# Two transformer blocks on one core: links between sublayers as one task of three parts, first group of the latent columns whole, weight sums in place

## The chip, the cores and the metric

The kernel runs on one core of one Trainium2 chip. The metric is the time of one execution on the device in microseconds (us), as the median of several runs. The engines are named as the profile names them: PE is TensorE (PEld its weight loads), DVE VectorE, ACT ScalarE, POOL GpSimd, SP SyncE.

## What is computed

The reference runs two blocks one after the other. The first holds two hybrid layers on 512 latent columns and 256 context columns of width 1024. Each layer is a feed-forward sublayer, a mixer (two kinds of attention and a Fourier transform between an input and an output projection), and a second feed-forward sublayer. Every sublayer takes the norm of its input, modulates it, and adds its normed and gated output to the input:

```python
def rms_norm(x, g):
    y = x32 * lax.rsqrt(jnp.mean(x32 * x32, axis=-1, keepdims=True) + RMS_EPS)
    return (y * g.astype(jnp.float32)).astype(x.dtype)

def ffn_sublayer(h, m, sub, g_pre, g_post, w1, w2):
    shift, scale, gate = mods_of(m, sub)
    y = swiglu(modulate(rms_norm(h, g_pre[sub]), shift, scale), w1, w2)
    return h + MACARON_WEIGHT * gate * rms_norm(y, g_post[sub])

def hybrid_layer(x, xc, mod, mod_c, ...):
    x = ffn_sublayer(x, mod, 0, g_pre, g_post, w_ffn_in[0], w_ffn_out[0])
    xc = ffn_sublayer(xc, mod_c, 0, g_pre, g_post, w_ffn_in[0], w_ffn_out[0])
    ...
    h = modulate(rms_norm(x, g_pre[1]), sh, sc)
    hc = modulate(rms_norm(xc, g_pre[1]), shc, scc)
    ...
    x = x + gt * rms_norm(o, g_post[1])
    x = ffn_sublayer(x, mod, 2, g_pre, g_post, w_ffn_in[1], w_ffn_out[1])
```

In the second layer the context ends after the mixer's input projection, which makes only keys and values of it. The second block (a linear recurrence with a state-space scan, then a stick-breaking attention) works on the latent columns and is not touched.

## The kernel before

Activations lie transposed: 128 features on the partitions, columns side by side, eight tiles for the width of 1024. The context columns are a stream named `cx` (256 columns, on the left), the latent ones `lat` (512), which is also cut into its halves `la` and `lb` (256 each). A float32 product is three matmuls (`mm3`, L421 to L423), of operands split in a high and a low part: ScalarE copies the high part (L347), VectorE or GpSimd subtracts it from the value (L353). Weights come through `raw` buffers (four, by DMA) and are split into `op` buffers (eight).

A feed-forward sublayer (`ffn`, named here by layer and place: 00, 02, 10, 12) goes through the hidden features in groups of 4, 4, 4, 3, 3 and 4 blocks. `ffn1` makes a group's hidden block (`mid`), `ffn2` adds its product to the output `Y`. In the first group ffn1 runs for cx, then for la, then for lb, each with its own load and split of the weights, because the columns of a sublayer come ready in that order. From the second group on, ffn1 of all 768 columns is done by a Strassen step over halves of 384 columns (`strassen`), seven products instead of eight; `wsums` makes the sums of weight blocks that it needs, four adds on VectorE for each block, into two buffers named `ws` and back into `raw`. The column sums that Strassen needs (`Halves`: `sums`, `third`) are made on VectorE and GpSimd beside the end of the first group. In the last group ffn2 runs for cx, then for lat.

Between two sublayers lies a link for each stream: `post` (norm of the output, gate, residual; L507, L509) and `pre` (norm of the new input, modulation and split; L525 to L527). Each of them calls `rstd`: two small matmuls of 128 x 1 sum the squares of 256 columns (L463), VectorE works out the reciprocal root on 128 x 2 values in 13 small steps (L474 to L482) and spreads it as a diagonal `dg` (L484), and two matmuls with it (L489) bring it to all partitions. The squares are added up by `add_sq` (L450) in a tile `ss`.

What order these pieces have on an engine is set when the program is built, by a small planner, `run`: tasks are generators that yield after each piece the time that it is thought to take (positive: TensorE's time, which moves the clock; negative: a time after which the task may go on). `run` takes next the first task whose time has come, the critical ones ahead of the fill. It returns when all are done (`drain`). The link of cx runs beside ffn2 of lat; the link of lat (at the borders into the mixers one link of 512 columns, at those out of the first mixer and of 02 the halves la and lb) runs in the next sublayer beside its first work on cx: ffn1 and ffn2 of the first group, or the mixer's context projections. TensorE runs its instructions in the order written; so does each other engine.

## Time and profile before

| | us |
|---|---|
| median of 3 runs | 3797.84 |
| the three runs | 3793.26 to 3799.57 |
| the profiled execution | 3801.48 |
| its span in the trace | 3799.7 |
| PE, DVE, ACT, POOL busy in it | 3504.7, 2364.0, 1708.1, 1400.0 |

The span is that of one execution seen by the hardware profiler, and the profiled execution's own time is some 2 us longer. "Busy" is the time in which an engine has an instruction under way, over the whole program; stretches with different limits are mixed in it, so that the sections below look at single borders between sublayers. PEclk in the rows is the clock granted to TensorE as a share of full speed: 1.00 is 2.4 GHz, 0.50 is 1.2 GHz.

### The profile page before, as it was taken

What the parts mean: (1) busy time and instruction counts of PE and PEld (TensorE: products, weight loads), DVE (VectorE), ACT (ScalarE), POOL (GpSimd) and SP (SyncE); (2) the same over time, 40 slices, a digit from 0 to 9 for tenths busy, and PEclk for the clock granted to TensorE, in tenths of its full rate; (3) what the DMA queues carried; (4) which work ended last, traced back from release to release, by engine and by line L of the source; (5) the groups of instructions that cost most, each with busy time, mean ns of one, the idle gap of its engine ahead of it and who ended that gap; (6) DMA issues with size and microseconds to landing.
All of it is one profiled execution on the core that took longest, in us unless ns stands there. A gap on an engine that the chain in (4) does not pass through costs nothing.

```text
span 3799.7 us, 61164 instructions
## 1 busy us (share of the span) xinstructions
PE 3504.7 (92%) x23260; PEld 3128.4 (82%) x23260; DVE 2364.0 (62%) x4769; ACT 1708.1 (45%) x3599; POOL 1400.0 (37%) x1151
## 2 busy tenths in 40 slices
PE   7899998998979999988999979888998898999997
PEld 5788897777878888888889967688887877999886
DVE  5844458667784444786445586667567776555546
ACT  5433334456543323454323445554444635635544
POOL 4533343211344333345333431145555433333112
PEclk8999998999989999999999989999999989999998
DMA  7433424212344343443342321242333311234112
GB/s 270 136 125 128 136 75 142 91 56 86 118 127 134 122 134 122 145 145 98 126 138 72 129 91 51 69 133 80 101 99 118 119 44 48 76 116 136 60 48 76
DMA packets 125437, 410.38 MB, mean 108 GB/s; under 512 B 14035, under 2 KB 25814, under 8 KB 123350
## 3 DMA queue, kind: packets, MB, share of 16 engines
q1 hardware_dynamic: 125142, 406.47, 33.5%
q8 instruction: 182, 2.98, 0.3%
q14 instruction: 113, 0.93, 0.1%
HBM read 397.90 MB, written 8.52 MB: 107 GB/s over the span
## 4 chain that ended last, share of the span: by engine, by line
PE 53%; DVE 15%; issue 5%; ACT 5%; POOL 2%; DMA 1%; ACTq 0%; DVEq 0%; POOLq 0%; SPq 0%
PE pg L421 9%; PE pg L422 9%; PE pg L423 9%; PE bank L416 7%; PE bank L421 4%; PE bank L423 3%; PE bank L422 3%; DVE op L353 2%; DVE ss L450 1%; PE po L611 1%; POOL op L353 1%; ACT op L347 1%; PE po L844 1%; PE psw L868 1%; PE po L1830 1%
## 5 line engine op out<-in xcount | busy, mean ns | idle before, releaser
L353 POOL TENSOR_TENSOR op<-raw,op 128x512 fp32r<-128x512 f32 (+1 forms) x660 | 891.2, 1351 | 1488.2 <-ACT op L347 1259.1
L347 ACT CAST op<-raw 128x512 fp32r<-128x512 f32 (+2 forms) x1178 | 709.9, 606 | 821.8 <-PE pg L423 421.3
L353 DVE TENSOR_TENSOR op<-raw,op 128x512 fp32r<-128x512 f32 (+2 forms) x518 | 402.6, 779 | 224.2 <-ACT op L347 217.7
L421 PE MATMUL pg<-h,op 128*128 128x256 f32 (+1 forms) x1440 | 480.1, 333 | 61.7 <-DVE m L758 26.5
L422 PE MATMUL pg<-h,op 128*128 128x256 f32 (+1 forms) x1440 | 467.9, 325 | 4.6 <-DVE h L527 3.3
L423 PE MATMUL pg<-h,op 128*128 128x256 f32 (+1 forms) x1440 | 462.3, 321 | 1.0 <-DVE op L353 0.6
L421 PE MATMUL pg<-mid,op 128*128 128x512 f32 (+1 forms) x1106 | 386.3, 349 | 13.6 <-ACT mid L347 5.3
L422 PE MATMUL pg<-mid,op 128*128 128x512 f32 (+1 forms) x1106 | 379.2, 343 | 1.8 <-DVE mid L353 1.7
L423 PE MATMUL pg<-mid,op 128*128 128x512 f32 (+1 forms) x1106 | 378.8, 342 | 0.0
L421 PEld LDWEIGHTS pg<-h,op 128*128 128x128 f32 x1440 | 293.6, 204 | 86.7 <-DVE m L758 29.2
L422 PEld LDWEIGHTS pg<-h,op 128*128 128x128 f32 x1440 | 292.7, 203 | 23.2 <-DVE h L527 11.1
L423 PEld LDWEIGHTS pg<-h,op 128*128 128x128 f32 x1440 | 293.1, 204 | 16.0 <-DVE op L353 1.0
L416 PE MATMUL bank<-h,op 128*128 128x384 f32 (+1 forms) x1704 | 293.5, 327 | 9.4 <-DVE u L704 9.4
L353 POOL TENSOR_TENSOR op<-ws,op 128x512 fp32r<-128x512 f32 x142 | 191.7, 1350 | 276.8 <-ACT op L347 276.8
L416 PEld LDWEIGHTS bank<-h,op 128*128 128x128 f32 x1704 | 280.9, 190 | 12.3 <-DVE u L704 12.3
L421 PEld LDWEIGHTS pg<-mid,op 128*128 128x128 f32 x1106 | 208.4, 188 | 75.0 <-DVE y L788 29.2
L788 DVE TENSOR_TENSOR y<-pg,y 128x256 f32<-128x256 f32 (+1 forms) x252 | 141.1, 562 | 198.2 <-PE pg L423 197.6
L422 PEld LDWEIGHTS pg<-mid,op 128*128 128x128 f32 x1106 | 208.6, 189 | 27.0 <-DVE mid L353 3.5
L423 PEld LDWEIGHTS pg<-mid,op 128*128 128x128 f32 x1106 | 208.3, 188 | 26.1
L421 PE MATMUL bank<-h,op 128*128 128x384 f32 (+1 forms) x636 | 206.4, 324 | 0.0
L423 PE MATMUL bank<-h,op 128*128 128x384 f32 (+1 forms) x636 | 203.6, 320 | 0.0
L422 PE MATMUL bank<-h,op 128*128 128x384 f32 (+1 forms) x636 | 203.6, 320 | 0.0
(434 smaller groups left out, 8430.1 us busy)
## 6 DMA issues: line engine op xcount, KB each, us to landing
raw<-wf SPq DMA_DIRECT2D x326, 512.0 KB, 3.7
mraw<-wmod SPq DMA_DIRECT2D x128, 512.0 KB, 4.7
raw<-win SPq DMA_DIRECT2D x58, 512.0 KB, 3.7
raw<-ewin SPq DMA_DIRECT2D x48, 512.0 KB, 3.6
raw<-owin SPq DMA_DIRECT2D x40, 512.0 KB, 3.6
raw<-wout SPq DMA_DIRECT2D x32, 512.0 KB, 3.6
raw<-wf SPq DMA_DIRECT2D x32, 384.0 KB, 3.2
raw<-ewout SPq DMA_DIRECT2D x24, 512.0 KB, 3.6
```

The source lines that it names most:

```text
L347: self.nc.scalar.copy(hi, src)
L353: eng.tensor_tensor(out=lo, in0=src, in1=hi.bitcast(F32), op=ALU.subtract)
L416: mm = self.nc.tensor.matmul if not more else lambda *a, **kw: self.nc.tensor.matmul(*a, skip_group_check=True, **kw)
L421: mm(p, lhsT=a, rhs=xh, start=start and i == 0, stop=False)
L422: mm(p, lhsT=a, rhs=xl, start=False, stop=False)
L423: mm(p, lhsT=b, rhs=xh, start=False, stop=stop and i == len(rhs) - 1)
L450: (eng or self.nc.vector).tensor_tensor(out=st.s, in0=st.s, in1=q, op=ALU.add)
L611: nc.tensor.matmul(box["po"][32 * j : 32 * j + 32, :], lhsT=self.cT[:, k, :], rhs=raws[j // 2][:, 512 * (j % 2) : 512 * (j % 2) + 512], st ...
L788: nc.vector.tensor_tensor(out=y, in0=p, in1=y, op=ALU.add)
L844: self.nc.tensor.matmul(o[64 * h : 64 * h + 64, :P], lhsT=cur["v"][h][c], rhs=pTs[h][:, c * P : (c + 1) * P], start=c == 0, stop=c == nt - 1)
L868: nc.tensor.matmul(S[:, h, col : col + ap.shape[1]], lhsT=q[h], rhs=ap, start=True, stop=True)
L1830: nc.tensor.matmul(o[64 * h : 64 * h + 64, :P], lhsT=vt[:m, t, 64 * h : 64 * h + 64], rhs=wTs[h][:m, t, :], start=t == 0, stop=t == j + 1)
```

## The change

Five things change together.

1. **Links as one task.** The links of cx, la and lb become one task, one after the other (`links`). It starts beside the last products of the sublayer and is carried over the border into the next one: `run` gets an `until`, with which it returns as soon as the fill is done and leaves the critical task where it stands. Notes order it: a link waits for the note "y" of its stream, set behind the stream's last product; the next sublayer's first work waits for the note "hcx", set behind cx's link.
2. **Last group in three parts.** ffn2 of the last group, and the first mixer's output projection, run for cx, la, lb (256 columns each) instead of cx, lat. So la's link may start beside lb's products. All links are of 256 columns now, into the mixers too.
3. **First group's latent part whole.** ffn1 of the first group runs for cx and then for all 512 latent columns at once, so that its weights are loaded and split twice instead of three times. At the start of the program the norm of the latent input is of 512 columns as well.
4. **Weight sums in place.** `wsums` writes three of its four sums over the weights in `raw` and one into a single `ws`.
5. **Small things.** Sum-of-squares tiles of up to 384 columns get buffers of their own (`sh`, 3), the wide ones one (`ss`); the 512-wide gate tile comes from the general buffers; the rotary tables are loaded when the first latent half is done with, or at the end of the entry.

The sublayer 12, the second block, and the exits from the second mixer keep their form. Line numbers of the helpers go down by one (L421 to L420, L463 to L462, L489 to L488).

```diff
-    def run(self, crit, fill=(), drain=True):
+    def run(self, crit, fill=(), drain=True, until=None):
         tasks = [t if isinstance(t, Task) else Task(t) for t in (*crit, *fill)]
-        must = tasks if drain else tasks[: len(crit)]
+        must = tasks[len(crit) :] if until else tasks if drain else tasks[: len(crit)]
         for t in tasks:
-            t.t = self.clock
+            t.t = max(t.t or 0, self.clock)
...
     def stile(self, n):
-        return self.tmp.tile([P, 512], F32, name="ss", tag="ssum", bufs=NSS)[:, :n]
+        return self.tmp.tile([P, 512], F32, name="ss", tag="ssum", bufs=1)[:, :n] if n > 384 else self.tmp.tile([P, 272], F32, name="sh", tag="sh", bufs=NSS)[:, :n]
...
         o1 = put(a11, True)
-        s1, s2 = tmp(), tmp()
+        s1 = self.fpool.tile([P, 512], F32, name="ws", tag="ws", bufs=1)
         add(s1, a21, a22)
         o2 = put(s1, True)
-        add(s2, s1, a11)
-        o3 = put(s2, False)
         add(a21, a11, a21)
+        add(a11, s1, a11)
+        o3 = put(a11, False)
         o4 = put(a21, True)
         o5 = put(a12, False)
-        add(s2, s2, a12)
-        o6 = put(s2, True)
+        add(a12, a11, a12)
+        o6 = put(a12, True)
         o7 = put(a22, True)
...
                 if first:
-                    self.run(pend[:1], [self.chain(g1(firsts[:1]), *([g2(firsts[:1], False)] if len(firsts) > 2 else []))])
-                    for i in range(1, len(firsts) - 1):
-                        self.run(pend[i : i + 1], [g1(firsts[i : i + 1], t=l == sub == 0)])
+                    self.run([pend], [self.chain(*([self.wait_for("hcx"), g1(firsts[:1]), g2(firsts[:1], False)] if full else [g1(firsts[:1])]))])
...
                     else:
-                        for i in range(len(lasts)):
-                            self.run(exits[i - 1 : i], [g2(lasts[i : i + 1], False, spill and not i and (lambda: spill(False)))])
+                        self.run([g2(lasts[:1], False, lambda: spill(False))])
+                        links = self.links(lasts, exits)
+                        self.run([links], [self.chain(*[x for st in lasts[1:] for x in (g2([st], False), self.mark(st, "y"))])], until=True)
+                        return links
...
+    def links(self, ss, exits):
+        self.known.pop("hcx", None)
+        self.yfree = False
+        def go():
+            for i, (st, e) in enumerate(zip(ss, exits)):
+                if i:
+                    yield from self.wait_for((st, "y"))
+                    del self.known[st, "y"]
+                yield from e
+                if not i:
+                    self.note("hcx")
+        return Task(go())
...
-            self.run([entry()], [proj(cx, [0, 1, 2, 7, 5, 6, 3, 4])])
+            self.run([entry()], [self.chain(self.wait_for("hcx"), proj(cx, [0, 1, 2, 7, 5, 6, 3, 4]))])
...
-                self.run(exits[:1], [o_proj(lat)])
+                links = self.links([cx, *lasts], exits)
+                self.run([links], [self.chain(*[x for st in lasts for x in (o_proj(st), self.mark(st, "y"))])], until=True)
+                return links
...
-        first = [cx, la, lb]
-        pend = [self.chain(self.square_x(st), self.pre(st, 0, 0)) for st in (la, lb)]
-        pend = self.ffn(0, 0, first, [lat], both, both, pend, links(0, 0, 0, 1), lambda out: spill(out, True), first=loads)
+        self.note("hcx")
+        pend = Task(self.chain(self.square_x(lat), self.pre(lat, 0, 0)))
+        pend = self.ffn(0, 0, both, [lat], both, parts, pend, links(0, 0, 0, 1), lambda out: spill(out, True), first=loads)
```

How this moves the instructions is seen in three places. The first is TensorE at the border from 02 to 10. Before, `bank<-ones,ss` and `bank<-dg,ones` are the sums and the diagonal of a norm, `h_122` to `h_129` the eight tiles of the new input (256 wide: context or one latent half), and `op` the weights. Around the sums of lb's first norm, and then (behind "...") around lb's second norm, stands:

```order
L423 MATMUL pg<-h_125,op 128x256
L421 MATMUL pg<-h_126,op 128x256
L422 MATMUL pg<-h_126,op 128x256
L423 MATMUL pg<-h_126,op 128x256
L463 MATMUL bank<-ones,ss 128x1 x2
L421 MATMUL pg<-h_127,op 128x256
L422 MATMUL pg<-h_127,op 128x256
L423 MATMUL pg<-h_127,op 128x256
...
L421 MATMUL pg<-h_129,op 128x256
L422 MATMUL pg<-h_129,op 128x256
L423 MATMUL pg<-h_129,op 128x256
L463 MATMUL bank<-ones,ss 128x1 x2
L489 MATMUL bank<-dg,ones 128x128 x2
L421 MATMUL pg<-h_122,op 128x256
```

Now the rows around lb's two norms on TensorE at the same border are these (`mid` is the context's hidden block, of ffn2):

```order
L420 MATMUL pg<-mid,op 128x256
L421 MATMUL pg<-mid,op 128x256
L422 MATMUL pg<-mid,op 128x256
L462 MATMUL bank<-ones,sh 128x1 x2
L420 MATMUL pg<-mid,op 128x256
L421 MATMUL pg<-mid,op 128x256
L422 MATMUL pg<-mid,op 128x256
L488 MATMUL bank<-dg,ones 128x128 x2
L462 MATMUL bank<-ones,sh 128x1 x2
L488 MATMUL bank<-dg,ones 128x128 x2
L420 MATMUL pg<-h_122,op 128x512
L421 MATMUL pg<-h_122,op 128x512
```

Before, la's first-group products (`h`, 128x256) stand around and between lb's norms; now three context products stand within the first norm and nothing behind it, and the next latent product, 512 wide, follows lb's second diagonal.

The second place is TensorE at the entry into the second mixer. Before, the end of the context projections and the norm of all 512 latent columns (`psw`, four matmuls each), with transposed values (`pt`) between, is:

```order
L950 MATMUL pt<-ident,vt 128x128 x2
L421 MATMUL pg<-h_129,op 128x256
L422 MATMUL pg<-h_129,op 128x256
L423 MATMUL pg<-h_129,op 128x256
L950 MATMUL pt<-ident,vt 128x128 x2
L463 MATMUL psw<-ones,ss 128x1 x4
L489 MATMUL psw<-dg,ones 128x128 x4
L421 MATMUL pg<-h_122,op 128x512
L422 MATMUL pg<-h_122,op 128x512
```

Now there are three norms of 256 columns in the same place, la's second and lb's two, the last two of which have nothing in front of them:

```order
L982 MATMUL pt<-ident,vt 128x128 x2
L420 MATMUL pg<-h_129,op 128x256
L421 MATMUL pg<-h_129,op 128x256
L422 MATMUL pg<-h_129,op 128x256
L488 MATMUL psw<-dg,ones 128x128 x2
L982 MATMUL pt<-ident,vt 128x128 x2
L462 MATMUL psw<-ones,sh 128x1 x2
L488 MATMUL psw<-dg,ones 128x128 x2
L462 MATMUL psw<-ones,sh 128x1 x2
L488 MATMUL psw<-dg,ones 128x128 x2
L420 MATMUL pg<-h_122,op 128x512
```

The latent projection (`h_122`, 128x512) follows directly behind lb's two norms, where one norm stood directly ahead of it before.

The third place is VectorE in two Strassen steps of the first sublayer. Before, the adds of `wsums` (L393) read `ws` and `raw` and write `ws` mostly, beside sums of results (L788) and splits (L353):

```order
L393 TENSOR_TENSOR ws_4361<-raw_4355 128x512
L393 TENSOR_TENSOR raw_4355<-raw_4354,raw_4355 128x512
L788 TENSOR_TENSOR y2_132<-pg_4040,y2_132 128x256
L788 TENSOR_TENSOR y2_132<-pg_4051,y2_132 128x512
L353 TENSOR_TENSOR op_4221<-ws_4215,op_4221 128x512
L788 TENSOR_TENSOR y3_133<-pg_4062,y3_133 128x256
L393 TENSOR_TENSOR ws_4215<-ws_4215,raw_4207 128x512
L788 TENSOR_TENSOR y3_133<-pg_4073,y3_133 128x512
L788 TENSOR_TENSOR y4_134<-pg_4100,y4_134 128x256
L788 TENSOR_TENSOR y4_134<-pg_4111,y4_134 128x512
L353 TENSOR_TENSOR op_4228<-raw_4207,op_4228 128x512
L788 TENSOR_TENSOR y5_135<-pg_4122,y5_135 128x256
```

Now (L392, with L815 for L788) they write `raw`:

```order
L392 TENSOR_TENSOR raw_3138<-ws_3145,raw_3138 128x512
L392 TENSOR_TENSOR ws_3293<-raw_3287 128x512
L392 TENSOR_TENSOR raw_3287<-raw_3286,raw_3287 128x512
L815 TENSOR_TENSOR y2_132<-pg_2935,y2_132 128x256
L815 TENSOR_TENSOR y2_132<-pg_2949,y2_132 128x512
L353 TENSOR_TENSOR op_3152<-raw_3138,op_3152 128x512
L815 TENSOR_TENSOR y3_133<-pg_2963,y3_133 128x256
L815 TENSOR_TENSOR y3_133<-pg_2977,y3_133 128x512
L815 TENSOR_TENSOR y4_134<-pg_3007,y4_134 128x256
L815 TENSOR_TENSOR y4_134<-pg_3021,y4_134 128x512
L353 TENSOR_TENSOR op_3158<-raw_3138,op_3158 128x512
L392 TENSOR_TENSOR raw_3138<-raw_3138 128x512
```

The add that makes `raw_3138` from `ws` and itself overwrites the weights' first piece, which the split into `op` must have read by then.

## Rows read from the trace of the kernel before

**Rows 1.** The page, busy time, share and instructions of each engine.

```profile
PE 3504.7 (92%) x23260; PEld 3128.4 (82%) x23260; DVE 2364.0 (62%) x4769; ACT 1708.1 (45%) x3599; POOL 1400.0 (37%) x1151
```

In the windows below stand: start and end, length, busy time (and instructions) of PE, PEld, DVE, ACT and POOL in this order, PEclk, the DMA engines' share and GB/s.

**Rows 2.** Windows at the border 02 to 10, cut at the diagonals.

```profile
1578.40:1604.20 25.80, 19.06 (x86) 15.13 (x84) 25.10 (x54) 11.93 (x24) 7.73 (x7) 0.93 0.37 127
1604.20:1616.60 12.40, 10.59 (x43) 9.45 (x44) 10.02 (x31) 4.93 (x11) 1.27 (x1) 0.50 0.20 76
1616.60:1641.00 24.40, 22.65 (x185) 22.24 (x184) 20.94 (x47) 12.70 (x28) 12.24 (x10) 0.98 0.51 151
1641.00:1660.70 19.70, 16.25 (x131) 15.68 (x131) 16.63 (x38) 12.16 (x29) 7.72 (x6) 1.00 0.40 135
1660.70:1685.20 24.50, 20.24 (x155) 19.98 (x155) 20.89 (x49) 12.08 (x27) 10.81 (x9) 0.93 0.73 236
1685.20:1729.00 43.80, 29.99 (x198) 27.79 (x199) 40.76 (x64) 20.52 (x44) 20.91 (x16) 0.84 0.27 87
1729.00:1756.00 27.00, 24.75 (x99) 19.11 (x98) 20.07 (x25) 10.55 (x21) 13.46 (x10) 0.94 0.18 59
```

**Rows 3.** Windows from the first mixer to 02, cut alike.

```profile
959.40:1006.00 46.60, 45.44 (x220) 37.21 (x219) 32.48 (x79) 26.01 (x51) 13.05 (x11) 1.00 0.42 136
1006.00:1033.40 27.40, 24.93 (x198) 24.72 (x197) 22.59 (x52) 14.61 (x32) 12.68 (x11) 0.94 0.48 144
1033.40:1050.40 17.00, 14.67 (x123) 14.30 (x121) 16.39 (x35) 11.83 (x27) 9.45 (x6) 1.00 0.40 140
1050.40:1076.40 26.00, 20.17 (x152) 19.71 (x152) 21.19 (x51) 12.64 (x27) 11.19 (x9) 0.90 0.74 231
1076.40:1124.00 47.60, 34.96 (x199) 32.72 (x200) 42.70 (x67) 20.46 (x43) 22.67 (x17) 0.73 0.28 86
1124.00:1147.00 23.00, 22.64 (x99) 18.08 (x98) 16.81 (x21) 10.40 (x21) 11.62 (x9) 1.00 0.15 47
```

**Rows 4.** Windows of the entries into the first and second mixer, from the latent diagonal.

```profile
637.40:689.40 52.00, 47.65 (x383) 47.03 (x383) 44.18 (x66) 29.60 (x58) 24.01 (x18) 0.96 0.42 135
2218.60:2252.70 34.10, 24.25 (x183) 23.34 (x181) 28.36 (x51) 15.88 (x31) 16.51 (x11) 0.90 0.49 159
2252.70:2257.20 4.50, 2.12 (x9) 1.83 (x9) 2.30 (x4) 0.82 (x2) 0.00 (x0) 0.50 0.01 2
```

**Rows 5.** Windows at the start: first group of la and lb.

```profile
82.00:114.00 32.00, 32.00 (x266) 29.62 (x268) 22.71 (x49) 18.46 (x40) 15.67 (x13) 1.00 0.60 198
114.00:148.00 34.00, 22.35 (x163) 20.04 (x156) 31.39 (x47) 15.39 (x32) 19.05 (x14) 0.90 0.54 179
```

**Rows 6.** Windows of a Strassen step and of 512-wide products.

```profile
1980.00:1996.00 16.00, 16.00 (x94) 14.91 (x93) 5.83 (x10) 6.16 (x13) 8.15 (x7) 1.00 0.46 140
2386.10:2403.10 17.00, 17.00 (x76) 13.68 (x75) 3.06 (x5) 7.73 (x11) 3.40 (x3) 1.00 0.28 87
```

**Rows 7.** Waits of PE, 1578 to 1730, 82 to 148, 2178 to 2258: total, times, longest.

```profile
PE bank L489 <- DVE dg L484: 11.2, 3, 4.6
...
PE pg L421 <- DVE m L758: 10.4, 2, 7.2
...
PE pt L950 <- ACT vt L995: 7.3, 3, 4.6
```

**Rows 8.** VectorE's groups over the span: busy us, mean ns, idle before and releasers.

```profile
L353 DVE TENSOR_TENSOR op<-raw,op 128x512 fp32r<-128x512 f32 x461 | 369.3, 803 | 196.0 <-ACT op L347 192.2
...
L450 DVE TENSOR_TENSOR ss<-ss,sq 128x256 f32<-128x256 f32 x136 | 85.5, 629 | 19.5 <-ACT sq L449 10.6 <-POOL ss L450 6.9
...
L393 DVE TENSOR_TENSOR ws<-raw 128x512 f32<-128x512 f32 x71 | 52.4, 737 | 189.4 <-POOL op L353 150.1 <-DMA raw<-wf 39.4
...
L450 DVE TENSOR_TENSOR ss<-ss,sq 128x512 f32<-128x512 f32 x36 | 26.0, 722 | 0.6 <-ACT sq L449 0.2
...
L525 DVE SCALAR_TENSOR_TENSOR u<-x,modA,bank 128x256 f32<-128x256 f32 x56 | 24.6, 475 | 6.0 <-PE bank L489 6.0
...
L481 DVE TENSOR_TENSOR v<-v 128x2 f32<-128x2 f32 x93 | 18.0, 193 | 3.1
```

More of the change, by code (lines that the diff above doesn't have):

```diff
@@ L511, in post @@
             yield -(0.4 + 1.5 * f)
-        self.yfree = True
+        if st.c0 < NL <= st.c0 + st.n:
+            self.yfree = True
         yield -1.72 * (2.2 + 1.8 * f)
@@ L666, in ffn @@
             self.fpool = self.sums = pool
+            full = len(lasts) > 2
             self.open_wide(True)
@@ L682, in ffn @@
                     h = Halves(self, pool, width // 2)
-                    self.run([h.sums()], [g1(firsts[-1:], t=l == sub == 0)])
+                    self.run([h.sums()], [g1(firsts[-1:], l == sub == 0)])
                     self.run([h.third()], [g2(parts, False)])
@@ L689, in ffn @@
                     elif lag:
-                        lg = lambda ss: self.chain(g1(ss, kg - lag), g2(ss, False))
+                        lg = lambda ss: self.chain(g1(ss, False, kg - lag), g2(ss, False))
                         self.run([lg(lasts[:1])])
@@ L698, in ffn, with own_y, mark @@
         return exits[-1]
+    def own_y(self, st):
+        st.y = lambda k: self.Y[k][:, st.cs]
+        return
+        yield
+    def mark(self, *what):
+        self.note(what)
+        return
+        yield
+    def links(self, ss, exits):
[10 more added lines that the diff above has]
+        return Task(go())
     def strassen(self, pool, l, wi, i0, mids, h):
@@ L927, in mix, with tables @@
             NB = [(Y[k][:, 256:512], Y[k][:, 512:768]) for k in (1, 2)]
-            self.yfree = False
             self.open_wide()
             def entry():
-                for v in pend:
+                for v in pend.gen:
                     if self.yfree and entry.first:
                         entry.first = False
-                        self.dma(cos, I["rope"][:, :NL])
-                        self.dma(sin, I["rope"][:, NL:])
+                        tables()
                     yield v
+                if entry.first:
+                    entry.first = False
+                    tables()
             entry.first = True
+            def tables():
+                self.dma(cos, I["rope"][:, :NL])
+                self.dma(sin, I["rope"][:, NL:])
             def vt(kind, i, base, t, offs):
@@ L1188, in mix @@
                 cx.y = lambda k: src[k][:, cx.cs]
+                exits[0] = self.chain(exits[0], self.own_y(cx))
             self.run([attention()], [side])
@@ L1240, in block1 @@
         link = lambda st, l, sub, l2, sub2: self.chain(self.post(st, l, sub, st), self.pre(st, l2, sub2))
-        def half(st, *a):
-            st.s = lat.s[:, st.c0 : st.c0 + 256]
-            yield from link(st, *a)
-        halves = lambda *a: [half(la, *a), half(lb, *a)]
-        links = lambda *a: [link(st, *a) for st in both]
+        parts = [cx, la, lb]
+        links = lambda *a: [link(st, *a) for st in parts]
         self.mod_setup()
@@ L1264, in block1 @@
         self.bg, loads = self.mods([((0, q), (0, q + 1)) for q in (2, 4, 6)])
-        first = [cx, la, lb]
-        pend = [self.chain(self.square_x(st), self.pre(st, 0, 0)) for st in (la, lb)]
-        pend = self.ffn(0, 0, first, [lat], both, both, pend, links(0, 0, 0, 1), lambda out: spill(out, True), first=loads)
+        self.note("hcx")
+        pend = Task(self.chain(self.square_x(lat), self.pre(lat, 0, 0)))
+        pend = self.ffn(0, 0, both, [lat], both, parts, pend, links(0, 0, 0, 1), lambda out: spill(out, True), first=loads)
         assert not self.bg
-        pend = self.mix(0, both, both, pend, [link(cx, 0, 1, 0, 2), halves(0, 1, 0, 2)])
+        pend = self.mix(0, both, [la, lb], pend, links(0, 1, 0, 2))
         self.bg, loads = self.mods([((0, 8), (1, 0)), ((1, 1), (1, 2)), ((1, 3), (1, 4))])
-        pend = self.ffn(0, 2, first, [lat], both, both, pend, [link(cx, 0, 2, 1, 0), halves(0, 2, 1, 0)], spill, first=loads)
+        pend = self.ffn(0, 2, both, [lat], both, parts, pend, links(0, 2, 1, 0), spill, first=loads)
         assert not self.bg
         self.bg, loads = self.mods([((1, 5), (1, 6)), ((1, 7), (1, 8))])
-        pend = self.ffn(1, 0, first, [lat], both, both, pend, links(1, 0, 1, 1), spill, first=loads)
+        pend = self.ffn(1, 0, both, [lat], both, parts, pend, links(1, 0, 1, 1), spill, first=loads)
         assert not self.bg
@@ L1878, in block2 @@
         self.wide.close()
-NSS = 2
+NSS = 3
 NOP = 8
```

8 lines of the change are left out of this document (3 added, 5 removed).

## Prediction

> **What bounds the kernel now.** I read the page first: TensorE is busy for 92% of the span, VectorE for 62% [rows 1]. Inside a feed-forward sublayer nothing is to be had: in a piece of the Strassen part TensorE is busy all the time and VectorE for 5.8 of 16 us [rows 6]. So I cut the span at the borders between sublayers, and there the picture turns. At the border from the second to the third feed-forward sublayer VectorE is busy for 154 of 177.6 us, the seven rows together, and TensorE has long gaps and drops to half clock (PEclk 0.50) after them [rows 2]. What VectorE does there is the "link": residual add, norm and modulation of the 256 context columns (cx), then of the 512 latent columns, here in two halves la and lb. Each of the three links holds two norms (`post` and `pre`), and each norm calls for TensorE twice: two tiny matmuls that sum squares, then two with a diagonal (`dg`). TensorE takes its instructions in program order, so it stands at each until VectorE has made the diagonal: 11.2 us in three waits at this border [rows 7]. The windows of rows 2 to 4 are cut at these diagonals, two to a link: the first window of rows 2 begins at the context's first, the third at la's first, the sixth at lb's second.
>
> **The change, part by part**, against the profiled execution (3801.48 us, span 3799.7), which is 3.64 above the median of 3797.84.
>
> *Matmul counts.* 256-wide latent matmuls become 512-wide in the three first groups (3 x 384 become 3 x 192), and 512-wide ones become 256-wide in three last groups and in one output projection (480 become 960). A 256-wide one issues every 0.12 us (266 in 32.0) [rows 5], a 512-wide one every 0.224 to 0.236 (76 in 17.0, of which four only reach in) [rows 6]. Net under 3 us, taken as nothing. What counts is who waits.
>
> *Start.* Before, la's and lb's first-group matmuls run from 82 to 148 us; the second 34 us hold 163 matmuls, with VectorE busy for 31.4 [rows 5] and TensorE waiting 10.4 us for it [rows 7]: the weights are loaded and split a second time while the Strassen sums run. Now one pass of 192 wide matmuls: 192 x 0.236 = 45.3, plus two small steps of the modulation's own matmuls, an estimate of 1 us each, from 82 to about 130; two other such steps move into the Strassen part (2 us by the same estimate). The latent norm is now one 512-wide piece and should be ready at about 82, since it has no first half to wait for. 148 - 130 - 2 = **16 saved**. Bounds: 19 if it starts without a wait, 6 if VectorE holds the pass up as it does now (34 us for 163 of 256 columns; half of the excess of 34 - 163 x 0.12 = 14 remains, and the start slips by 3).
>
> *Border two to three (feed-forward to feed-forward).* The order of the links in TensorE's queue stays as it was up to la's; lb's two norms now stand at the end of cx's first group, with nothing between them and the latent pass that needs them, as the rows of order above show. (a) The context link runs beside two 256-wide parts instead of one 512-wide: 16 square-adds of 0.63 for 8 of 0.72, and 4 more weight splits of 0.8 [rows 8], +4.3 + 3.2 = 7.5, and the evacuations of results add a little in the same way. In the three windows up to la's second diagonal VectorE has 0.7 + 2.4 + 3.5 = 6.6 idle; I let these hide all but 2.5 (0 to 9 uncovered). (b) From la's first diagonal to its second, 24.4 us, TensorE has 180 matmuls to issue, 22 at full rate; unchanged. (c) From there to lb's first, 19.7 becomes 14: the rest of the context's first group (63 matmuls, 8 us) is all that TensorE has in front, and VectorE has 16 link operations of 0.475, 13 tiny ones of 0.19 and 3 splits of 0.8 [rows 8], 12.5 in all; hand-offs between engines add the rest. (d) From there to lb's second, 24.5 becomes 15: the pieces of la's first group leave VectorE (6 small ones and 7 splits of 0.8, 8 of its 20.9 us), and 12.5 with hand-offs stay. So lb's diagonal comes 2.5 - 5.7 - 9.5 = 12.7 earlier. (e) From it to the end of the pass was 43.8 us; now it is 3 to the first matmul (from a latent diagonal to it took up to 4.5 [rows 4]), 45.3, and 4 for the half clock after the wait, since 12.4 us at PEclk 0.50 follow such a wait [rows 2] and I take 8 of them here, of which half is lost: 52.3, +8.5. So the pass ends 4.2 earlier. (f) The piece behind it, 27.0, took 23.0 at the other border, where VectorE had 16.8 to do instead of 20.1 [rows 2, 3]; half of it, 2, I give. **6 saved.** Bounds: 15 saved without the clock loss, with (a) at nothing and (f) whole; 9 lost if (c) and (d) stay as they are (2.5 + 8.5 - 2).
>
> *First mixer to second feed-forward.* The same, and la's link no longer waits for the whole latent projection to end: la's diagonal comes 42 us behind the context's instead of 46.6 (276 matmuls x 0.12 = 33 in front, and I allow 9 for waits). Then 27.4, 17.0 and 26.0 [rows 3] become 22.5 (180 matmuls), 15.5 and 17.5, so lb's diagonal comes 4.5 + 4.9 + 1.5 + 8.5 = 19 earlier. From there 52.3 where it was 47.6: 14.3 saved, less 1.5 for the doubled weight splits of the projection, as far as VectorE's idle time there doesn't hide them: **13 saved** (20 to 2).
>
> *Into the two mixers.* Here the link of 512 columns becomes two of 256 in series, and the cover does not grow: context projections alone. First mixer: 52.0 us from the latent diagonal to the projection's end [rows 4]; now 22 (180 matmuls) to la's second diagonal, 14 and 17 to lb's two and 3 to the first latent matmul: 56, so +4; +2.5 as in (a); +2.5 for half clock after the waits: **9 lost** (0 to 22). Second mixer, where only half of the projections exist: 34.1 + 4.5 [rows 4] against 22.5 + 10.5 (no splits beside it) + 14 + 2.5 = 49.5, +11, and +2.5, with up to 2 of clock: **15 lost** (5 to 35).
>
> *Weight sums in place.* Four adds per block as before. One now overwrites the weights and must wait until GpSimd has subtracted the first piece; the order shows it a whole Strassen step ahead of its matmul. That VectorE waits here is nothing new: 150.1 us for GpSimd before the first add of 71 blocks, 2.1 each [rows 8], while TensorE is busy for 16.0 of 16.0 [rows 6]. **Nothing**, covered by the 10 us that VectorE is idle in a step; without that cover 71 x 2.1 = 149. The Trainium skill speaks against this edit: "TensorE: Matmul & The Clock Gate", section "Architectural detail", says that VectorE's queue is strictly first in, first out, so whatever stands behind a waiting add waits too. By that rule alone the sum would be 149 us worse; the rows say that the wait is there already and costs TensorE nothing.
>
> Sum: -16 - 6 - 13 + 9 + 15 = -11: 3790.5 for an execution like the profiled one, 3787 on the median's scale.
>
> **The rivals.** (1) *Mixer entries cost nothing*: la's values are ready some 12 us sooner, so la's and lb's links could end behind the projections. For: in the second entry TensorE waits 7.3 us for transposed values [rows 7], time that a link could use. Against: one task runs the three links one after the other, so la's still begins when cx's ends. Then -35: 3763. (2) *The wide pass is set by VectorE*: weight splits, evacuations and 512-wide pieces all pass through it, and from lb's diagonal on it is busy for 40.8 of 43.8 and 42.7 of 47.6 us now [rows 2, 3]. If each of three wide passes takes 5 to 8 more, the sum is -11 + 15 to 24 = +4 to +13: about 3806. (3) *Slower by the links in halves*: if (c) and (d) stay at 19.7 + 24.5 = 44.2 wherever lb's link runs without cover, the mixers lose 9 + 13 = 22 and 15 + 20 = 35, the second border loses 9 and the first saves 3: -16 + 9 - 3 + 22 + 35 = +47, 3845. For it: the trace shows just these stretches, with VectorE busy in most of them. Against: the matmuls and splits that made it busy are gone. It decides as soon as the two stretches between la's second diagonal and lb's second last 3 us longer together, at each of the four borders, than used here (-11 + 4 x 3 = +1). (4) *The in-place add stalls TensorE*: if the wait moves from where VectorE is idle to where a matmul needs it, up to +149, 3935 and more; for it speaks only that the add's wait ends later in a step than the old one did.
>
> **How the numbers follow.** Forecast 0.46 (own range 3776 to 3800), (1) 0.17, (2) 0.15, (3) 0.18, (4) 0.04. The three runs spread by 6.3 us, so 0.2%, 7.6 us, is about what can be told from no change: faster means below 3790.2, slower above 3805.4. Of the forecast 0.28 lies below and 0.18 within; (1) below; (2) 0.08 within and 0.07 above; (3) and (4) above. Faster 0.45, same 0.26, slower 0.29. The range takes in the forecast, (1) down to 3762, (2), and the near third of (3), up to 3822; what it leaves out is 0.12 of (3), (4) and 0.03 of (1).
>
> **What would show it.** In the profile after: one pass of 192 wide matmuls from 82 to 130 at the start; at the second border the latent pass begins some 97 us after the context link's first diagonal (106.8 before to lb's second diagonal, and some 3 more) and goes on for under 52; at the first, it ends about 14 us nearer to that diagonal; in the mixers the first latent matmul comes some 58 and 52 us behind the latent columns' first diagonal (52.0 and 38.6 before); the Strassen steps last 16 us as before. The forecast is wrong if the wide pass shows TensorE waiting for VectorE for more than 8 us, if more than 35 us pass from la's second diagonal to lb's second, or if the Strassen step grows.

## The result and the profile after

The changed kernel takes 3841.45 us (median of 4 runs, 3837.7 to 3842.52), the kernel before 3795.55 in the same comparison: a ratio of 1.0118, 95% interval 1.0101 to 1.0136. It is some 46 us slower, where the prediction's sum was 11 us less. The page's first lines of the profiled execution after:

```profile
span 3840.4 us, 61074 instructions
PE 3479.7 (91%) x23164; PEld 3098.6 (81%) x23164; DVE 2443.9 (64%) x4888; ACT 1705.6 (44%) x3623; POOL 1406.0 (37%) x1149
```

Against [rows 1] TensorE is busy for 25 us less and yet the span is 41 us longer: some work has gone, some matmuls issue faster, and more waiting has come. Where, is seen from landmarks that all kernels share: the first and last matmul of each Strassen part on TensorE (384 wide, in sublayer 12 256 wide), which cut the program into stretches with one border or mixer each (us, from the traces; the runs in the last four columns are told below).

| stretch | before | after | a_two | b_halves | a_slowsums | best_b |
|---|---|---|---|---|---|---|
| start to the first Strassen part | 170.6 | 157.1 | 158.4 | 169.2 | 152.6 | 152.9 |
| 00 to 02, with the first mixer | 565.3 | 591.4 | 577.0 | 579.0 | 583.0 | 551.9 |
| border 02 to 10 | 194.5 | 200.5 | 194.5 | 190.9 | 193.1 | 186.7 |
| 10 to 12, with the second mixer | 463.5 | 486.3 | 475.8 | 476.9 | 484.0 | 463.3 |
| Strassen parts of 00, 02, 10 | 1230.7 | 1219.3 | 1219.3 | 1230.9 | 1219.3 | 1219.3 |
| from 12's Strassen part to its end | 269.3 | 280.9 | 279.1 | 269.4 | 278.6 | 271.3 |
| the rest | 905.8 | 904.9 | 905.8 | 905.7 | 910.7 | 903.6 |

After against before: -13.5 + 26.1 + 6.0 + 22.8 - 11.4 + 11.6 - 0.9 = +40.7, the difference of the spans. So the start is near its forecast, each border has lost, and two rows moved that the prediction had held still. Each column is one execution, and a stretch moves between executions: 00 to 02 took 561.2, 557.8 and 560.9 us in three runs that leave it as it was before (b_wsums, b_start and w_pad32, told below), so the 565.3 of the kernel before is 4 to 8 us high and the loss there rather 30 to 34 than 26. The windows of the border 02 to 10 after, cut at the same diagonals as [rows 2]:

```profile
1586.80:1615.70 28.90, 19.50 (x155) 18.60 (x155) 28.29 (x67) 14.64 (x35) 11.54 (x9) 0.95 0.53 177
1615.70:1627.70 12.00, 9.52 (x51) 8.39 (x52) 10.35 (x32) 5.48 (x12) 1.28 (x1) 0.69 0.20 83
1627.70:1651.10 23.40, 21.33 (x178) 20.72 (x176) 21.13 (x49) 12.14 (x28) 12.48 (x10) 1.00 0.53 160
1651.10:1669.00 17.90, 12.17 (x86) 11.77 (x86) 13.70 (x36) 10.39 (x25) 5.41 (x4) 0.86 0.31 102
1669.00:1683.80 14.80, 2.21 (x8) 1.85 (x8) 10.32 (x35) 3.31 (x8) 2.60 (x3) 0.50 0.53 198
1683.80:1744.10 60.30, 50.43 (x197) 39.88 (x198) 41.67 (x64) 22.02 (x42) 22.70 (x17) 0.88 0.21 62
1744.10:1766.80 22.70, 22.22 (x98) 17.91 (x97) 16.95 (x21) 10.66 (x20) 11.76 (x9) 1.00 0.15 45
```

From the context's first diagonal to lb's second it is 97.0 us (forecast 94.1, before 106.8): the link did get shorter, and the pass's first matmul came 99.8 us behind that diagonal, where 97 were forecast. Two windows took it back: the first, in which VectorE is now busy for 28.3 of 28.9 us with 67 instructions instead of 54, and the sixth, the wide pass, 60.3 us where 43.8 stood. In the fifth TensorE has 8 matmuls in 14.8 us, at half clock (0.50). The first window also begins later, by the stretch from the end of the Strassen part to the context's first diagonal, here before and after:

```profile
1561.10:1578.40 17.30, 17.00 (x121) 15.46 (x120) 14.24 (x38) 9.21 (x19) 5.18 (x5) 1.00 0.85 292
```

```profile
1566.20:1586.80 20.60, 17.85 (x146) 17.06 (x144) 17.65 (x42) 12.03 (x25) 7.96 (x7) 1.00 0.74 255
```

The longest wait inside the wide pass is this row of the waits (1684 to 1744; total, times, longest):

```profile
PE pg L420 <- DVE m L785: 5.8, 1, 5.8
```

Out of the first mixer the windows after, cut like [rows 3] up to the end of the pass, are:

```profile
964.60:1008.90 44.30, 35.28 (x292) 34.59 (x292) 40.85 (x87) 26.21 (x63) 19.19 (x15) 1.00 0.56 183
1008.90:1036.50 27.60, 25.14 (x188) 24.93 (x188) 22.89 (x47) 15.64 (x33) 14.21 (x11) 0.88 0.48 146
1036.50:1051.70 15.20, 11.73 (x98) 11.56 (x98) 14.44 (x38) 8.72 (x19) 4.41 (x3) 1.00 0.31 99
1051.70:1073.40 21.70, 12.57 (x86) 12.14 (x86) 15.77 (x40) 10.24 (x25) 8.56 (x7) 0.77 0.77 248
1073.40:1133.30 59.90, 50.00 (x197) 39.57 (x198) 41.77 (x64) 22.02 (x42) 22.87 (x17) 0.89 0.20 62
```

Together they are 168.7 us, against 164.6 before: 4 lost where 13 were to be saved.

Into the mixers the same is seen without any cover. The windows of the second entry after, from la's first diagonal to the first latent matmul, 53.6 us together against 38.6 in [rows 4]:

```profile
2232.20:2257.60 25.40, 19.96 (x165) 19.18 (x163) 22.48 (x49) 13.29 (x31) 14.24 (x11) 1.00 0.53 171
2257.60:2268.50 10.90, 2.29 (x10) 2.21 (x10) 9.13 (x33) 4.06 (x8) 0.00 (x0) 0.51 0.18 48
2268.50:2283.00 14.50, 2.21 (x8) 1.86 (x8) 10.29 (x35) 3.33 (x8) 2.61 (x3) 0.50 0.13 37
2283.00:2285.80 2.80, 1.23 (x5) 0.94 (x5) 1.49 (x4) 0.57 (x2) 0.00 (x0) 0.50 0.00 0
```

For the last 28 of them TensorE has 23 matmuls, at half clock.

### The profile page after: what moved, and what is told of

The parts are those of the page before. It is cut to its first block, busy times and chain, and to the rows that moved or that the text cites. A ratio compares the mean times of both kernels' runs of the same rounds, so it can differ in the third digit from the quotient of the medians.

```text
span 3840.4 us, 61074 instructions
## 1 busy us (share of the span) xinstructions
PE 3479.7 (91%) x23164; PEld 3098.6 (81%) x23164; DVE 2443.9 (64%) x4888; ACT 1705.6 (44%) x3623; POOL 1406.0 (37%) x1149
## 5 line engine op out<-in xcount | busy, mean ns | idle before, releaser
L353 POOL TENSOR_TENSOR op<-raw,op 128x512 fp32r<-128x512 f32 (+1 forms) x727 | 973.2, 1341 | 1739.3 <-ACT op L347 1470.5
L347 ACT CAST op<-raw 128x512 fp32r<-128x512 f32 (+2 forms) x1312 | 789.2, 608 | 988.1 <-PE pg L422 536.1
L353 DVE TENSOR_TENSOR op<-raw,op 128x512 fp32r<-128x512 f32 (+2 forms) x585 | 453.8, 777 | 220.6 <-ACT op L347 216.6
L420 PE MATMUL pg<-h,op 128*128 128x256 f32 (+1 forms) x1312 | 448.0, 341 | 39.2 <-DVE m L785 22.1
L421 PE MATMUL pg<-h,op 128*128 128x256 f32 (+1 forms) x1312 | 436.7, 333 | 7.0 <-DVE h L527 5.5
L420 PE MATMUL pg<-mid,op 128*128 128x256 f32 (+1 forms) x1190 | 402.2, 338 | 35.0 <-DVE y L815 18.0
L422 PE MATMUL pg<-h,op 128*128 128x256 f32 (+1 forms) x1312 | 431.0, 329 | 3.1 <-DVE op L353 2.4
L421 PE MATMUL pg<-mid,op 128*128 128x256 f32 (+1 forms) x1190 | 392.7, 330 | 0.4 <-DVE mid L353 0.3
L422 PE MATMUL pg<-mid,op 128*128 128x256 f32 (+1 forms) x1190 | 392.1, 329 | 0.0
L420 PEld LDWEIGHTS pg<-h,op 128*128 128x128 f32 x1312 | 259.8, 198 | 67.5 <-DVE m L785 24.4
L420 PEld LDWEIGHTS pg<-mid,op 128*128 128x128 f32 x1190 | 226.7, 190 | 96.9 <-DVE y L815 32.0
L415 PE MATMUL bank<-h,op 128*128 128x384 f32 (+1 forms) x1704 | 288.9, 324 | 16.9 <-DVE u L731 16.9
L815 DVE TENSOR_TENSOR y<-pg,y 128x256 f32<-128x256 f32 (+1 forms) x273 | 144.1, 530 | 225.4 <-PE pg L422 225.3
L421 PEld LDWEIGHTS pg<-h,op 128*128 128x128 f32 x1312 | 259.5, 198 | 31.8 <-DVE h L527 14.5
L422 PEld LDWEIGHTS pg<-h,op 128*128 128x128 f32 x1312 | 259.3, 198 | 23.5 <-DVE op L353 2.8
L421 PEld LDWEIGHTS pg<-mid,op 128*128 128x128 f32 x1190 | 226.6, 190 | 21.1 <-DVE mid L353 2.3
L422 PEld LDWEIGHTS pg<-mid,op 128*128 128x128 f32 x1190 | 226.6, 190 | 20.7
L420 PE MATMUL bank<-h,op 128*128 128x384 f32 (+1 forms) x636 | 204.9, 322 | 0.0
L421 PE MATMUL bank<-h,op 128*128 128x384 f32 (+1 forms) x636 | 202.1, 318 | 0.0
L422 PE MATMUL bank<-h,op 128*128 128x384 f32 (+1 forms) x636 | 201.9, 317 | 0.0
L420 PE MATMUL pg<-ha,op 128*128 128x272 f32 (+1 forms) x552 | 169.0, 306 | 6.4 <-ACT u L1449 2.2
```

The lines of the kernel that those rows point to most:

```text
L347: self.nc.scalar.copy(hi, src)
L353: eng.tensor_tensor(out=lo, in0=src, in1=hi.bitcast(F32), op=ALU.subtract)
L415: mm = self.nc.tensor.matmul if not more else lambda *a, **kw: self.nc.tensor.matmul(*a, skip_group_check=True, **kw)
L420: mm(p, lhsT=a, rhs=xh, start=start and i == 0, stop=False)
L421: mm(p, lhsT=a, rhs=xl, start=False, stop=False)
L422: mm(p, lhsT=b, rhs=xh, start=False, stop=stop and i == len(rhs) - 1)
```

## The experiments

Each is the kernel before (names with b_, and w_, which has in-place sums besides) or the changed kernel (a_) with the edit shown. Ratios are to the kernel before, run beside each on the same chip (3796.7 to 3797.2 us).

**b_wsums**, weight sums in place alone: in `wsums` of the kernel before, the lines of the change's diff.

> The kernel before with the weight sums in place and one ws buffer, nothing else of the change. The prediction's working: nothing, within 3 us of before, in every Strassen step. The rival, from the trace after: in the narrow Strassen steps of sublayer 12 (256 columns a half, 11.3 us each) VectorE has no idle time to wait in, so the adds that now wait for GpSimd hold its queue; sublayer 12 grows by about 11 us and the steps of 16 us stay as they are: +11.

3809.70 us, 1.0031 (1.0019 to 1.0043): 12.5 more. The stretch of sublayer 12 takes 278.7 us instead of 269.3, the other Strassen parts 1233.0 instead of 1230.7 (b_start below, with the old sums, has 1232.9). The rival's size and place hold. The waits of sublayer 12's Strassen part show how; the kernel before (2625 to 2894), its window last:

```profile
DVE ws L393 <- POOL op L353: 43.7, 21, 6.2
PE bank L416 <- DVE u L704: 8.7, 10, 2.6
ACT op L347 <- DVE ws L393: 3.6, 2, 1.8
2625.00:2894.00 269.00, 255.78 (x1765) 235.99 (x1764) 161.92 (x269) 117.63 (x235) 159.32 (x124) 0.99 0.32 97
```

and the changed kernel (2655 to 2936):

```profile
ACT op L347 <- DVE raw L392: 50.2, 21, 4.6
DVE raw L392 <- POOL op L353: 28.7, 16, 7.7
PE bank L415 <- DVE u L731: 16.6, 11, 3.6
2655.00:2936.00 281.00, 255.30 (x1768) 234.95 (x1767) 179.45 (x270) 115.79 (x235) 156.92 (x124) 0.98 0.29 92
```

One add of each block now waits for GpSimd, ScalarE's copies wait for that add, 50 us where it was 4, and TensorE waits 16.6 us instead of 8.7 for the products' sums (`u`), which stand in VectorE's queue with the adds. But VectorE doesn't wait longer for GpSimd than before (28.7 us for this add, against 43.7 for the adds then), and it was not without idle time, as the rival had it: it was busy for 162 of 269 us. What has grown is its own work, by 17.5 us with one instruction more. In b_wsums the adds over the whole program are:

```profile
L392 DVE TENSOR_TENSOR raw<-raw 128x512 f32<-128x512 f32 x142 | 106.4, 749 | 3.7
L392 DVE TENSOR_TENSOR raw<-ws,raw 128x512 f32<-128x512 f32 x71 | 91.1, 1284 | 121.6 <-POOL op L353 121.6
```

The add that waits for GpSimd takes 1.28 us, the others of its shape 0.75. Worked out of the trace's records, 18 of these 71 ran with no GpSimd instruction under way and took 0.69 us each; 31 ran with one under way for over 70% of their time and took 1.43. So two costs stand side by side, the work that waits behind or for the add and the longer add itself, and no run separates them.

**a_ws12**, the other way round: the changed kernel with the old sums in sublayer 12 only.

```diff
+            self.inplace = len(joint) > 1
...
+        if not self.inplace:
+            tmp = lambda: self.fpool.tile([P, 512], F32, name="ws", tag="ws", bufs=2)
+            o1 = put(a11, True)
+            s1, s2 = tmp(), tmp()
...
```

> The changed kernel with the weight sums of the narrow Strassen steps in sublayer 12 alone as before the change (two ws buffers), in place elsewhere. If in-place sums cost only there: 9 to 12 us less, 3829 to 3832. If the loss in sublayer 12 comes from elsewhere: no change, 3841.

3831.19 us, 1.0085 (1.0071 to 1.0100): 10 less than the changed kernel. So the in-place sums' cost lies there: the interval of b_wsums (7 to 16 more) takes in these 10.

**b_start**, the start alone: `self.ffn(0, 0, both, ...)`, with the latent norm of 512 columns.

> The kernel before with the latent part of the first group whole in sublayer 00 alone, and the latent norm at the start in one piece of 512 columns. The prediction's working: 16 saved. By the trace after, where the first Strassen step begins 13.5 us earlier: 13 saved. The rival that VectorE sets the pass: 6 or less.

3790.61 us, 0.9981 (0.9972 to 0.9990): 7 less; in its trace the first Strassen part begins 11.2 us earlier. The gain is there, smaller by the time than both expectations (the interval reaches from 4 to 11 us less).

**b_whole**, that in all three sublayers, with la's and lb's links chained beside the context's first group:

```diff
-        halves = lambda *a: [half(la, *a), half(lb, *a)]
+        halves = lambda *a: [self.chain(half(la, *a), half(lb, *a))]
...
-        pend = self.ffn(1, 0, first, [lat], both, both, pend, links(1, 0, 1, 1), spill, first=loads)
+        pend = self.ffn(1, 0, both, [lat], both, both, pend, links(1, 0, 1, 1), spill, first=loads)
```

> The kernel before with the latent part of the first group whole in all three sublayers 00, 02 and 10; the links of la and lb both run beside the context's first group, none of the rest of the change. The prediction's working for this part: start 16, border two to three 6 + 2.5, first mixer to second feed-forward about 10 saved: some 34 less than before. The rival, that the wide pass is held up by VectorE and lb's link has lost its cover: the two borders gain nothing or lose up to 5 each, so 13 less to 3 less.

3793.03 us, 0.9980 (0.9970 to 0.9989), no better than b_start. The rival holds: at the two later borders the whole pass alone is worth nothing.

**a_mixlat**, the changed kernel with two parts and one latent link of 512 columns at the entries into the mixers, as before; the links stay one carried task:

```diff
...
-        pend = self.ffn(1, 0, both, [lat], both, parts, pend, links(1, 0, 1, 1), spill, first=loads)
+        pend = self.ffn(1, 0, both, [lat], both, both, pend, [link(st, 1, 0, 1, 1) for st in both], spill, first=loads)
```

> The changed kernel, but at the two borders from a feed-forward sublayer into a mixer the last group is in two parts (cx, lat) and the latent link is one of 512 columns, as before the change. The prediction's working priced these two borders at 9 and 15: 24 less than the changed kernel, 3817. The rival, by the landmarks of the two traces (21 lost at each): 42 less, about 3800. If neither halves nor parts matter there but the carrying over of the task: no change from 3841.

3794.34 us, 0.9990 (0.9982 to 0.9999): 47 less. These two borders hold the whole loss by the time, in two parts that the next two runs separate.

**b_halves**, the kernel before with the latent link into the mixers as two of 256 columns:

```diff
-        self.yfree = True
+        if st.c0 < NL <= st.c0 + st.n:
+            self.yfree = True
...
+        two = lambda *a: [link(cx, *a), self.chain(*halves(*a))]
...
-        pend = self.ffn(1, 0, first, [lat], both, both, pend, links(1, 0, 1, 1), spill, first=loads)
+        pend = self.ffn(1, 0, first, [lat], both, both, pend, two(1, 0, 1, 1), spill, first=loads)
```

> The kernel before with the latent link into the two mixers as two of 256 columns, one after the other, and nothing else (the last group still in two parts, nothing carried over a border). If the loss of 47 us at these borders is the second half link standing without cover: the second mixer loses 15 to 17 and the first 6 to 10, so 21 to 27 more than before, and the rest of the loss belongs to the three-part last group. The prediction's working for the same two steps, without the context link's 2.5 each: 19 more. If the halves cost nothing: no change.

3833.21 us, 1.0087 (1.0072 to 1.0101): 36 more by the time; in the profiled execution, at the low end of its five runs (3823.8 to 3839.4), 22 more in the span, 13.7 and 13.4 in the two mixer stretches. Its windows at the second entry, from la's second diagonal to lb's second, are those of the changed kernel:

```profile
2253.40:2264.00 10.60, 2.01 (x10) 1.93 (x10) 9.11 (x33) 4.07 (x8) 0.00 (x0) 0.54 0.15 51
2264.00:2278.50 14.50, 2.21 (x8) 1.85 (x8) 10.30 (x35) 3.33 (x8) 2.60 (x3) 0.50 0.13 37
```

So the halves alone do this, with nothing carried over and no third part.

**a_two**, the changed kernel with the last group and the first mixer's output projection in two parts, the task of three links kept:

```diff
-   links = self.links(lasts, exits)
-   self.run([links], [self.chain(*[x for st in lasts[1:] for x in (g2([st], False), self.mark(st, "y"))])], until=True)
+   links = self.links([lasts[0], *self.two], exits)
+   self.run([links], [self.chain(g2(lasts[1:], False), self.half_y(lasts[1]))], until=True)
...
```

> The changed kernel with the last group (and the first mixer's output projection) again in two parts, cx and lat, while the links stay one carried task of cx, la and lb; both latent halves are released when the whole latent product is done. If the three parts cost what the landmarks show around the context link (its diagonals come 6 to 7 us later at each border, against 2.5 in the prediction): about 20 less than the changed kernel, 3821. If la's later start takes that back: no change, 3841.

3807.80 us, 1.0027 (1.0018 to 1.0036): 34 less than the changed kernel, more than expected. By stretch it gives back 14.4 (two borders), 6.0 and 10.5: all that the border 02 to 10 had lost. Its first two windows there are those of [rows 2] again:

```profile
1570.40:1596.10 25.70, 18.72 (x86) 15.10 (x84) 25.07 (x53) 11.93 (x24) 7.75 (x7) 0.95 0.39 128
1596.10:1608.40 12.30, 10.41 (x46) 9.27 (x47) 9.71 (x32) 4.93 (x11) 1.27 (x1) 0.54 0.20 79
```

**a_slowsums**, the changed kernel with the column sums spread over the wide pass:

```diff
-            yield -4.5
+            yield -11 if self.n == XW // 2 else -4.5
```

> The changed kernel with the planner told that each of the four pieces of the column sums takes 11 us instead of 4.5 beside the wide latent pass, so that VectorE's queue holds the pass's own products ahead of later sums. If TensorE's 8.2 us of waits in the pass and the half clock after them come from products standing behind the sums (the rival that VectorE sets the wide pass): 5 to 8 us less in each of three passes, 3818 to 3826. If they come from weights being split too late: no change, 3841.

3819.63 us, 1.0055 (1.0043 to 1.0068): 22 less. The wide pass at the border 02 to 10, from its first matmul, in this kernel:

```profile
1674.20:1722.10 47.90, 47.08 (x194) 37.89 (x195) 41.52 (x60) 21.54 (x42) 21.91 (x17) 0.95 0.22 67
```

and in the changed kernel:

```profile
1686.60:1744.10 57.50, 49.23 (x193) 38.95 (x194) 40.25 (x61) 21.51 (x41) 22.70 (x17) 0.90 0.21 64
```

VectorE does nearly the same work in both (41.5 and 40.3 us): it was not too much, it stood in the wrong order. The wait of 5.8 us for `m` is gone; the longest that TensorE has left inside the pass is

```profile
PE pg L420 <- ACT h L526: 1.1, 1, 1.1
```

**w_pad1216** and **w_pad32**, b_wsums with an unused tile, to test where the 11.4 us in the Strassen parts come from that no edit explains:

```diff
+        self.nc.gpsimd.memset(self.tmp.tile([P, 304], F32, name="pad", tag="pad", bufs=1)[:, :1], 0.0)
```

(w_pad32: `self.const.tile([P, 8], ...)`, which comes first of all.)

> The kernel before with the weight sums in place (12 us above before, by the run of that part alone) and an unused tile of 1216 bytes per partition ahead of the temporary buffers, as much as the changed kernel's sum-of-squares tiles take more there; every activation tile moves by that much, the order of the instructions stays. In the changed kernel 384-wide matmuls issue every 0.1744 us, in the kernel before every 0.1768. If that comes from where the tiles lie: 0.1744 here too, some 4900 such matmuls give 12 us back and the 256-wide and 512-wide ones (0.002 to 0.003 us each) up to 10 more, so about 3790. If it comes from the order or from another part: 0.1768 and no change, 3810.

> As the run with the unused tile of 1216 bytes, but of 32 bytes and ahead of everything, so that weights and activations all begin at multiples of 128 bytes, where now they begin 32 bytes beside a multiple of 64. If a tile's place within 64 bytes is what counts: the 384-wide matmuls get at least as fast as 0.1744 us, 3790 or less. If it is not, and the interval depends on something coarser: anything from 0.1744 to 0.1768, up to 3810.

w_pad1216: 3795.47 us, 0.9991 (0.9983 to 1.0000), 14 less than b_wsums. w_pad32: 3812.01, 1.0035 (1.0022 to 1.0048), none. The group of 1296 Strassen matmuls (total busy, mean ns) in the kernel before, after, in w_pad1216 and in w_pad32:

```profile
L416 PE MATMUL bank<-h,op 128*128 128x384 f32 x1296 | 237.4, 338 | 0.7 <-DVE u L704 0.7
```

```profile
L415 PE MATMUL bank<-h,op 128*128 128x384 f32 x1296 | 234.0, 336 | 0.4 <-DVE u L731 0.4
```

```profile
L416 PE MATMUL bank<-h,op 128*128 128x384 f32 x1296 | 234.0, 336 | 0.5 <-DVE u L704 0.5
```

```profile
L416 PE MATMUL bank<-h,op 128*128 128x384 f32 x1296 | 237.2, 338 | 0.1
```

The gain goes with the shift of 1216 bytes alone. A tile's place within 64 bytes is not what counts; what does is open.

**best_a** and **best_b** put together what paid: wide passes with spread sums, in-place sums except in sublayer 12. best_a is a_mixlat with these two edits, best_b is b_whole with them and the 1216 bytes; in best_b this part of `ffn` and `wsums` differs from b_whole:

```diff
+            self.inplace = len(joint) > 1
...
-            yield -4.5
+            yield -11 if self.n == XW // 2 else -4.5
...
+        if self.inplace:
+            o1 = put(a11, True)
+            s1 = self.fpool.tile([P, 512], F32, name="ws", tag="ws", bufs=1)
...
```

> What the runs point to, from the changed kernel: 512-wide latent links and two-part last groups into the mixers (3794 by itself), column sums paced at 11 us (22 less), weight sums in place only in the sublayers with 16 us steps (9 to 12 less). If these add up: about 3762. If the pacing and the mixer links overlap: up to 3780.

> What the runs point to, from the kernel before: first group's latent part whole in three sublayers (3793 by itself), column sums paced at 11 us, weight sums in place only in the sublayers with 16 us steps, and the unused 1216 bytes (14 less). No three-part groups, nothing carried over a border. If these add up: about 3757. If the pacing helps only where a link is carried over: about 3779.

best_a: 3769.55 us, 0.9922 (0.9910 to 0.9935). best_b: 3750.34 us, 0.9870 (0.9857 to 0.9884), 47 us faster than before, with links that end at the border. The windows of best_b at the border 02 to 10:

```profile
1539.80:1565.80 26.00, 19.08 (x85) 15.46 (x84) 25.00 (x53) 11.93 (x24) 7.75 (x7) 0.89 0.39 130
1565.80:1578.30 12.50, 10.60 (x47) 9.45 (x48) 10.08 (x32) 5.01 (x12) 1.27 (x1) 0.54 0.18 67
1578.30:1601.80 23.50, 21.55 (x182) 21.14 (x180) 21.07 (x47) 12.62 (x28) 12.32 (x10) 1.00 0.52 157
1601.80:1619.80 18.00, 12.06 (x86) 11.66 (x86) 13.78 (x36) 10.32 (x25) 5.15 (x4) 0.86 0.31 104
1619.80:1634.30 14.50, 2.20 (x8) 1.85 (x8) 10.29 (x35) 3.31 (x8) 2.60 (x3) 0.50 0.54 203
1634.30:1684.80 50.50, 48.04 (x197) 38.70 (x198) 42.85 (x63) 22.02 (x42) 21.80 (x17) 0.92 0.22 64
```

The short link of the changed kernel is here too (18.0 + 14.5 in place of [rows 2]'s 19.7 + 24.5), since it comes from taking la's matmuls away; the first window has its old length and the pass takes 50.5 us.

## Why the prediction was wrong, step by step

**Part (a), the three-part last group, and (e) failed most.** Part (a) was priced at 2.5 us a border because VectorE's 6.6 idle us in the three windows up to la's second diagonal were let hide the rest. Those idle times lie behind the work to be hidden, inside a chain in which VectorE waits for TensorE; they cannot take work that the chain's first window already waits for, in which VectorE was busy for 25.1 of 25.8 us [rows 2] and is now for 28.3 of 28.9. The first window grew by 3.1 us and its start by another 3, and a_two shows what the parts cost over the program: 34 us, where 2.5 at three borders and 1.5 at the fourth had made 9.

**The halves into the mixers** had the right sign and mechanism and were too small: 19 us without (a), against 27 in the trace and 36 by the time of b_halves. In the changed kernel the second entry went as worked out but slower: 25.4, 10.9, 14.5 and 2.8 where 22.5, 10.5, 14 and 2.5 stood. So rival (1), that the entries cost nothing, falls. At the first entry the same four were 23.8, 14.5, 21.5 and 1.2 where 22, 14, 17 and 3 stood; the stretch between lb's diagonals was the one taken too short:

```profile
665.70:687.20 21.50, 13.43 (x86) 13.03 (x86) 15.13 (x43) 7.72 (x17) 6.50 (x6) 0.76 0.31 91
```

**(c) and (d)** were 14 and 15, and became 17.9 and 14.8 from 19.7 and 24.5: 11.5 of the 15.2 us came. So rival (3), whose 3845 lies nearest to the time, was right mostly by its sum: these stretches did not stay as they were. Its sign, 3 us more than forecast from la's second diagonal to lb's second, did come at three of the four borders (3.7 and 3.9 us behind 02 and the first mixer, 5.0 into the first mixer), but not at the fourth (0.9, into the second).

**(e), the wide pass**, was 52.3 from lb's diagonal and took 60.3, and 59.9 at the other border: that is rival (2), which gave 5 to 8 us a pass to VectorE. a_slowsums shows that the order of the work did it, and gave 22 us back; by the stretches 4.5, 8.4 and 7.4 at the three passes. At the border 02 to 10 forecast (6 saved) and trace (6 lost) then differ by 12 us: 4 from (a) with what lies ahead of its window, 4 from (c) and (d), 8 from (e), while (b), (f) and the second window gave 4 back. Out of the first mixer the forecast missed by 17 us: the pass is 7.6 longer than worked out, lb's stretch 4.2 (21.7 for 17.5), the way to la's first diagonal 2.3, and la's window took 27.6 us, as before, where 22.5 were expected.

**The start**: 16 forecast, 13.5 in the trace, the pass 54.8 us long instead of 48 for the same reason, but begun earlier. Alone, by the time, it is 7 (4 to 11), and 11.2 at the first Strassen part of b_start's trace; that trace, of the fastest of nine executions, has a span 16 us shorter than before and shows nothing that takes the gain back later.

**Weight sums in place**, priced at nothing, cost 10 to 12 us. The row used for it was of a step of 16 us in which VectorE is idle for 10 [rows 6]; the narrow steps of sublayer 12 were not looked at. What stands ahead of the prediction says that sublayer 12 keeps its form; its links do, but its weight sums are in place too. The rule that the prediction quoted from the Trainium skill ("TensorE: Matmul & The Clock Gate", section "Architectural detail", a strict queue on VectorE) agrees with the trace as far as it goes: TensorE's waits for the products' sums in that queue grew by 8 us. The 50 us of ScalarE are waits for the add's own result, VectorE's wait for GpSimd did not grow, and the add took longer beside GpSimd, which the prediction did not have. The 149 us of rival (4) did not come; in the wide steps the cover held.

**Not seen at all**: the faster matmuls, 14 us by w_pad1216, without which the change would have been slower still.

Together, by the stretches: -13.5 for the start, -11.4 for the matmuls in the Strassen parts, +11.6 for sublayer 12, and 54.9 at the borders, of which 30.9 are the three parts (a_two) and 27.1 the halves into the mixers (b_halves); the rest, -3, would be the gain that link and whole pass leave, but it is less than a stretch moves between executions. The two were measured in different surroundings, so the sum is a check and not a proof.

## What to carry to other kernels

In a link of dependent steps, idle time in a later window hides nothing of the work that a full earlier window waits for, and a chain that has lost its cover costs the waits and the half clock behind them. When work is cut into more pieces, or moved in place, look at the border or the step with the least idle time, not at the most common one. Before an engine is called the bound of a pass, ask in what order its queue holds the work: the same 41 us on VectorE made the pass 57.5 or 47.9 us long.

## What was not expected of the hardware

The same matmuls in the same order issue 1.4% faster when every activation tile lies 1216 bytes further on in SBUF (1296 of them busy for 234.0 us instead of 237.4; as the mean from start to start, worked out of the traces' matmul records, 0.1744 us instead of 0.1768 for 384 columns), worth 14 us of 3810. A shift of 32 bytes, which brings all tiles to multiples of 128 bytes, changed nothing (237.2). Which distance decides it stays open.

An add of 128x512 on VectorE takes 0.69 us with GpSimd idle and 1.34 to 1.43 us with GpSimd at work beside it (the in-place adds of the changed kernel and of b_wsums, worked out of the traces' records). In-place, the add starts when GpSimd ends one piece and has GpSimd's next beside it for two thirds of its time. The profile's times of GpSimd are rough, and no run tests what makes the add longer.
